# The second gate's column sums: from VectorE's multiply-adds to a ScalarE scale and a GpSimd add

## The chip, the core and the metric

The kernel runs on one core of a Trainium2 chip. The metric is the time of one execution on the device in microseconds (us), taken as the median of several runs. Five engines work side by side, each through its own queue of instructions in order: TensorE (PE: matmuls, with PEld for its weight loads), VectorE (DVE), ScalarE (ACT), GpSimd (POOL) and SyncE (SP, which here issues the loads). An instruction waits at the head of its queue until what it needs is there, and all behind it on that engine wait too.

## What is computed

One decoder block over 256 tokens of width 2048, all in float32. A conditioning vector c gives six vectors of 2048 numbers, and the last of them, the second gate g2, is what the change is about:

```python
mod = silu(c) @ w_ada + b_ada                      # (2048) @ (2048 x 12288)
sh1, sc1, g1, sh2, sc2, g2 = split(mod, 6)
h = rms_norm(x) * (1 + sc1) + sh1;  proj = h @ w_in
# ... attention on one half of the heads, a short gated convolution on the other
x = x + g1 * (mixed @ w_out)
h2 = rms_norm(x) * (1 + sc2) + sh2
u = causal_dwconv(h2 @ w_ffn_up);  u_gate, u_up = split(u, 2)
x = x + g2 * ((silu(u_gate) * u_up) @ w_ffn_down)
```

## The kernel before

**Slots.** The program is written as a row of slots. Each slot is one tile of weights (128 x 4 x 512 numbers, 1 MB) and the matmuls that use it. The slots are those of `w_in`, then `w_out`, then the feed-forward in four segments: of each segment the up projection (tiles named z) and then the down projection (tiles named m('D', segment, f)). A float32 weight tile is used as two halves: `split_hi` lets ScalarE write the upper half `hi` (L266), `split_lo` lets VectorE subtract it from the raw tile to get the lower half `lo` (L272). `hi` and `lo` have three buffers each. Slot i prepares the halves of slot i+2, so `lo` is made one to two slots ahead of the matmuls that read it.

**Loads.** Raw tiles (`raw`, six buffers) are loaded by SyncE in the order in which they will be used: when one has been used up, `load_next` issues the next load into the buffer that comes free.

**The six vectors (class Ada).** `w_ada` is loaded as raw tiles among the weights. A group of columns is summed up in one of two ways: on TensorE (L324), or as column sums on VectorE: for each of the 16 blocks of 128 rows, the tile times `csil` (one number per partition, silu(c)) is added to an accumulator of 128 partitions (L328, L330). Which slots take which tile is in a table (CFG['ada']). The second gate (part 5) is one group of 2048 columns: 16 tiles of 128 x 2048, each a raw tile of its own, spread over 21 slots from slot 103. Its accumulator takes one of the six raw buffers: `home` clears it on GpSimd and loads the bias into its row 0 (L308, L310). One multiply-add at L330 follows per tile.

**After the sums.** `halve` splits a quarter of the accumulator (512 columns) into halves, ScalarE (L347) and then VectorE (L348), and `spread` (L386, L387, L390) sums over the partitions with matmuls against ones. The first `halve` of the second gate stands in the slot after the last tile was added; the `spread`s come 21 slots later. Around it, in the up projection of the second segment, VectorE and ScalarE do the sums of a group (`up_sum`, L768, L771), its convolution (L734, L739) and its gating (L786, L790, L792, L793).

**The order inside slot i:** `split_hi` for slot i+2, the tasks of the slot, `split_lo` for slot i+2, the slot's matmuls, and then the Ada tiles of the slot (`consume`, L315). Some slots have `split_hi` after the tasks. No scheduler changes this: each engine runs its instructions as they are written.

Of the kernel before, what the change touches and what calls it, by code (L numbers as in the profile page):

```python
# [10 lines left out]
AF = mybir.ActivationFunctionType  # L11
ALU = mybir.AluOpType
# [15 lines left out]
SH1, SC1, G1, SH2, SC2, G2 = range(6)  # L28
# [106 lines left out]
def tile_block(  # L135
# [5 lines left out]
    nc = tc.nc  # L141
    mm = nc.tensor.matmul
    act = nc.scalar.activation
# [7 lines left out]
    def bank(name):  # L151
        return ps.tile([P, 512], F32, tag="b", bufs=8, name=name)
# [3 lines left out]
    def t2k(name, dt=F32):  # L156
        return sb.tile([P, 512], dt, tag="t2k", bufs=N_T2K, name=name)
# [7 lines left out]
    def t4k(name, dt=F32):  # L165
        return sb.tile([P, 1024], dt, tag="t4k", bufs=N_T4K, name=name)
# [61 lines left out]
    def load_next():  # L228
        if pending:
            if isinstance(pending[0], Ada):  # L230

                pending.pop(0).home()
                return
            t = sb.tile([P, 4, 512], F32, tag="raw", bufs=N_RAW, name="raw")
            pending.pop(0)(t)
            ready.append(t)

    def take():
        t = ready.pop(0)
        return t  # L240
# [36 lines left out]
    csil = const.tile([P, NK], F32, name="csil")  # L277
# [6 lines left out]
    class Ada:  # L284
# [30 lines left out]
        def consume(self, r):  # L315
            t = self.view(take())
            if r == 0 and self.acc is None:
                what = f"ada{self.part}_{self.c0}"
                self.acc = (bank(what) if self.pe else t4k(what) if self.n > 512 else t2k(what))[:, :self.n]
            for j in range(self.rows):  # L320
                i = self.rows * r + j
                if self.pe:
                    q = 32 * (j % 4)
                    mm(self.acc[q:q + 32, :], crep[:, i, :], t[:, j, :],  # L324
                       start=(r == 0 and j < 4), stop=(r == self.tiles - 1 and j >= self.rows - 4),
                       tile_position=(0, q))
                elif i == 0 and self.n <= 1024:
                    V.tensor_scalar(self.acc, t[:, j, :], csil[:, i:i + 1], None, op0=ALU.mult)  # L328
                else:
                    V.scalar_tensor_tensor(out=self.acc, in0=t[:, j, :], scalar=csil[:, i:i + 1],  # L330
                                           in1=self.acc, op0=ALU.mult, op1=ALU.add)
            load_next()
# [265 lines left out]
    for n, (f, part, k) in enumerate(seq):  # L598
# [6 lines left out]
        i = len(slots)  # L605
# [519 lines left out]
    for half in range(2):  # L1125
        for w in "qk":
            at(in_last[f"{w}{half}"], qk_stat, f"{w}{half}")
        i = max(in_last[f"{w}{half}"] for w in "qk")
# [274 lines left out]
```

## Time and profile before

| | |
|---|---|
| median of 3 runs | 1172.55 us (1172.13 to 1173.67) |
| span of the profiled execution | 1170.4 us |
| what the runs' median has beyond that span | 2.2 us |
| PE / PEld busy | 1151.1 / 973.6 us |
| DVE busy | 921.9 us |
| ACT busy | 626.3 us |
| POOL busy | 12.0 us |
| loads | 318 MB, mean 272 GB/s |

The page gives the span of one profiled execution, from its first instruction to its last; the runs' times lie 2.2 us above it. All comparisons of stretches below are in us from the start of that span. A row of a group reads: line, engine, operation, output<-inputs, shapes, count | busy us, mean ns of one | idle time of the engine just before them, and who ended it. A row of the timeline reads: start, duration, engine, line, operation; in brackets how long the engine was idle before it and what it waited for. Durations hold a small tail that overlaps with the next instruction of the same engine.

### The profile page before, as it was taken

The page shows a single profiled execution, that of the slowest core. Times are in us where ns is not written, and L with a number is a line of the kernel's source. Part 1 is how long each engine was busy: PE and PEld are TensorE (multiplying, and loading weights), DVE is VectorE, ACT ScalarE, POOL GpSimd, SP SyncE. Part 2 cuts the span into 40 slices and gives each one's busy share as a digit, 9 for nine tenths or more (in the row PEclk, how much of TensorE's full clock was granted, in tenths as well). Part 3 has the DMA queues.
Part 4 walks back from the last instruction along what each step waited for, and adds up shares of the span by engine and source line. Part 5 has one row for each costly group of instructions (what it writes and reads, how often), then busy time and mean ns, then how long its engine had stood idle before and what let it go on. Part 6 is the DMA issues. An engine that isn't in the chain of part 4 may idle for free.

```text
span 1170.4 us, 15668 instructions
## 1 busy us (share of the span) xinstructions
PE 1151.1 (98%) x6115; PEld 973.6 (83%) x6115; DVE 921.9 (79%) x1030; ACT 626.3 (54%) x906; POOL 12.0 (1%) x24
## 2 busy tenths in 40 slices
PE   5999999999999999999999999999999999999998
PEld 3777778888888889988888888888888888888886
DVE  3889989999999978899876767986556576478766
ACT  6645365567785564666664444555444554336441
POOL 1000000000000000000000000000000000000000
PEclk9999999999999999999999999999999999999999
DMA  9999989999899799975555898984664646675441
GB/s 364 406 415 411 409 321 372 378 349 347 287 332 350 251 326 331 359 253 178 186 194 168 305 337 301 310 279 154 208 222 159 201 162 216 222 252 168 150 162 73
DMA packets 189052, 318.00 MB, mean 272 GB/s; under 512 B 7073, under 2 KB 105845, under 8 KB 184625
## 3 DMA queue, kind: packets, MB, share of 16 engines
q1 hardware_dynamic: 187232, 314.60, 75.6%
q10 hardware_dynamic: 1296, 2.16, 0.5%
q8 instruction: 48, 0.79, 0.3%
q0 software_dynamic: 448, 0.24, 0.1%
q14 instruction: 28, 0.22, 0.1%
HBM read 312.77 MB, written 4.19 MB: 271 GB/s over the span
## 4 chain that ended last, share of the span: by engine, by line
PE 91%; DVE 3%; ACT 2%; DMA 2%; issue 1%; SPq 0%; DVEq 0%; ACTq 0%
PE z L875 24%; PE z L878 13%; PE z L861 4%; DVE lo L272 1%; PE ada L324 1%; PE mk L443 1%; PE mk L444 1%; PE mk L441 1%; PE mq L443 1%; PE mq L444 1%; PE mq L441 1%; PE mx L443 1%; PE mc L443 1%; PE mx L444 1%; PE mc L444 1%; PE mv L443 1%
## 5 line engine op out<-in xcount | busy, mean ns | idle before, releaser
L272 DVE TENSOR_TENSOR lo<-raw,hi 128x2048 fp32r<-128x2048 f32 (+2 forms) x201 | 445.9, 2224 | 140.4 <-ACT hi L266 135.5
L266 ACT ACTIVATE hi<-raw 128x2048 fp32r<-128x2048 f32 (+2 forms) x201 | 373.8, 1865 | 311.9 <-PE z L875 60.2
L875 PE MATMUL z<-h,hi 128*128 128x512 f32 x1280 | 299.0, 390 | 0.2 <-DVE h L696 0.2
L875 PEld LDWEIGHTS z<-h,hi 128*128 128x128 f32 x1280 | 237.6, 188 | 48.1 <-PE z L875 0.6
L330 DVE SCALAR_TENSOR_TENSOR ada<-raw,csil,ada 128x512 f32<-128x512 f32 (+3 forms) x167 | 195.4, 1175 | 5.6 <-DMA raw<-in_w_ada_dram 2.1
L878 PEld LDWEIGHTS z<-h,lo 128*128 128x128 f32 x1280 | 159.3, 192 | 3.4
L878 PE MATMUL z<-h,lo 128*128 128x256 f32 x1280 | 160.5, 283 | 0.0
L739 DVE SCALAR_TENSOR_TENSOR uy<-ub,fc,uy 128x254 f32<-128x254 f32 (+1 forms) x176 | 71.3, 476 | 0.2
L771 DVE TENSOR_TENSOR ub<-z,ub 128x256 f32<-128x256 f32 x96 | 33.9, 415 | 37.9 <-ACT ub L768 37.9
L792 ACT ACTIVATE gh<-uy 128x512 fp32r<-128x512 f32 x22 | 13.9, 632 | 62.9 <-DVE uy L790 62.9
L861 PE MATMUL z<-h,hi 128*128 128x256 f32 x256 | 46.6, 284 | 0.4 <-ACT h L693 0.2
L734 ACT ACTIVATE uy<-ub,fc,fc 128x256 f32<-128x256 f32 x88 | 45.6, 602 | 0.0
L768 ACT ACTIVATE ub<-z 128x256 f32<-128x256 f32 x96 | 28.8, 384 | 31.4 <-PE z L875 31.4
L861 PEld LDWEIGHTS z<-h,hi 128*128 128x128 f32 x256 | 40.0, 192 | 0.8 <-ACT h L693 0.5
L861 PE MATMUL z<-h,lo 128*128 128x256 f32 x128 | 36.2, 283 | 0.0
L324 PE MATMUL ada<-raw,crep 128*32 128x256 f32 (+1 forms) x192 | 20.3, 535 | 7.9 <-DMA raw<-in_w_ada_dram 7.9
L793 DVE TENSOR_TENSOR gl<-uy,gh 128x512 fp32r<-128x512 f32 x22 | 15.2, 692 | 15.4 <-ACT gh L792 15.4
L443 PE MATMUL mq<-hi,h 128*128 128x512 f32 x64 | 25.5, 398 | 0.4 <-DVE adaz L361 0.4
L443 PE MATMUL mx<-hi,h 128*128 128x512 f32 x64 | 25.7, 401 | 0.0
L443 PE MATMUL mc<-hi,h 128*128 128x512 f32 x64 | 25.6, 400 | 0.0
L443 PE MATMUL mk<-hi,h 128*128 128x512 f32 x64 | 25.1, 393 | 0.0
L443 PE MATMUL mv<-hi,h 128*128 128x512 f32 x64 | 25.1, 392 | 0.0
(612 smaller groups left out, 1885.4 us busy)
## 6 DMA issues: line engine op xcount, KB each, us to landing
raw<-in_w_ada_dram SPq DMA_DIRECT2D x96, 1024.0 KB, 6.8
raw<-in_w_ffn_up_dram SPq DMA_DIRECT2D x176, 512.0 KB, 4.5
raw<-in_w_in_dram SPq DMA_DIRECT2D x47, 1024.0 KB, 7.8
raw<-in_w_ffn_down_dram SPq DMA_DIRECT2D x28, 1024.0 KB, 5.0
raw<-in_w_out_dram SPq DMA_DIRECT2D x16, 1024.0 KB, 6.0
raw<-in_w_ffn_down_dram SPq DMA_DIRECT2D x20, 768.0 KB, 4.2
xr<-in_x_dram SPq DMA_DIRECT2D x2, 1024.0 KB, 6.4
x<-in_x_dram SPq DMA_DIRECT2D x8, 256.0 KB, 6.6
```

What stands on the lines that cost most here:

```text
L266: act(hi[:, :nk], t[:, :nk], AF.Copy)
L272: V.tensor_tensor(out=lo[:, :nk], in0=t[:, :nk], in1=hi[:, :nk].bitcast(F32), op=ALU.subtract)
L324: mm(self.acc[q:q + 32, :], crep[:, i, :], t[:, j, :], start=(r == 0 and j < 4), stop=(r == self.tiles - 1 and j >= self.rows - 4), tile_p ...
L330: V.scalar_tensor_tensor(out=self.acc, in0=t[:, j, :], scalar=csil[:, i:i + 1], in1=self.acc, op0=ALU.mult, op1=ALU.add)
L443: mm(o, a, hi[:, k, s], start=(first and k == 0), stop=False)
L444: mm(o, b, hi[:, k, s], start=False, stop=False)
L734: act(y[:, s], b[:, s], AF.Identity, bias=bias[:, i + j:i + j + 1], scale=w[2][:, i + j:i + j + 1])
L739: V.scalar_tensor_tensor(out=o[:, d:], in0=v[:, :256 - d], scalar=w[2 - d][:, i + j:i + j + 1], in1=o[:, d:], op0=ALU.mult, op1=ALU.add)
L771: V.tensor_tensor(out=d, in0=zp[grp][ft][:, :256], in1=d, op=ALU.add)
L861: mm(o, w[:, j, a], h2T[k + j][:, v * 256:v * 256 + 256], start=begins and j == 0 and w is hi and not v, stop=ends and j == 3 and w is lo)
L875: mm(zp[grp][ft], hi[:, j, ft * P:(ft + 1) * P], h2T[k + j], start=begins and j == 0, stop=ends and j == 3)
L878: mm(zp[grp][ft][:, :256], lo[:, j, ft * P:(ft + 1) * P], h2T[k + j][:, :256], start=False, stop=False)
```

## The change

For tiles of the second gate alone, `consume` issues two instructions in place of one: ScalarE multiplies the raw tile in place by silu(c), and GpSimd adds it to the accumulator. The accumulator, the loads, their order and everything after the sums stay as they are. Lines behind the change have numbers higher by 3 in the new kernel.

```diff
                 elif i == 0 and self.n <= 1024:
                     V.tensor_scalar(self.acc, t[:, j, :], csil[:, i:i + 1], None, op0=ALU.mult)
+                elif self.part == G2:
+                    act(t[:, j, :], t[:, j, :], AF.Copy, scale=csil[:, i:i + 1])
+                    nc.gpsimd.tensor_tensor(out=self.acc, in0=self.acc, in1=t[:, j, :], op=ALU.add)
                 else:
                     V.scalar_tensor_tensor(out=self.acc, in0=t[:, j, :], scalar=csil[:, i:i + 1],
                                            in1=self.acc, op0=ALU.mult, op1=ALU.add)
```

Two places show how the instructions move. The first is ScalarE's queue at the end of the sums, before the change; `adah` is the upper half that the first `halve` writes, `ada_0_5668` the accumulator, `ub` and `uy` are tiles of the up projection's sums and convolution, `gh` an upper half of the gated result:

```order
L266 ACTIVATE hi<-raw 128x2048
L734 ACTIVATE uy_6567<-ub_6506,fc_1676,fc_1672 128x256 x2
L734 ACTIVATE uy_6568<-ub_6507,fc_1676,fc_1672 128x256 x2
L266 ACTIVATE hi<-raw 128x2048 x2
L347 ACTIVATE adah<-ada_0_5668 128x512
L786 ACTIVATE uy_6567<-uy_6567 128x512
L792 ACTIVATE gh_6673<-uy_6567 128x512
L266 ACTIVATE hi<-raw 128x2048
```

The same stretch of ScalarE's queue after the change:

```order
L266 ACTIVATE hi<-raw 128x2048
L737 ACTIVATE uy_6581<-ub_6519,fc_1676,fc_1672 128x256 x2
L737 ACTIVATE uy_6582<-ub_6520,fc_1676,fc_1672 128x256 x2
L330 ACTIVATE raw<-raw,csil 128x2048
L266 ACTIVATE hi<-raw 128x2048
L330 ACTIVATE raw<-raw,csil 128x2048
L266 ACTIVATE hi<-raw 128x2048
L350 ACTIVATE adah<-ada_0_5668 128x512
L789 ACTIVATE uy_6581<-uy_6581 128x512
L795 ACTIVATE gh_6689<-uy_6581 128x512
L266 ACTIVATE hi<-raw 128x2048
```

The scales (now at L330) stand between the weight splits, each behind the `hi` of its own slot; the first `adah` is still behind all of them, and now it needs the last add of GpSimd. The second place is VectorE's queue at the same point, before:

```order
L330 SCALAR_TENSOR_TENSOR ada_0_5668<-raw,csil,ada_0_5668 128x2048
L272 TENSOR_TENSOR lo<-raw,hi 128x2048
L739 SCALAR_TENSOR_TENSOR uy_6567<-ub_6506,fc_1668,uy_6567 128x255 x2
L739 SCALAR_TENSOR_TENSOR uy_6567<-ub_6506,fc_1664,uy_6567 128x254 x2
L739 SCALAR_TENSOR_TENSOR uy_6568<-ub_6507,fc_1668,uy_6568 128x255 x2
L739 SCALAR_TENSOR_TENSOR uy_6568<-ub_6507,fc_1664,uy_6568 128x254 x2
L330 SCALAR_TENSOR_TENSOR ada_0_5668<-raw,csil,ada_0_5668 128x2048
L272 TENSOR_TENSOR lo<-raw,hi 128x2048
L330 SCALAR_TENSOR_TENSOR ada_0_5668<-raw,csil,ada_0_5668 128x2048
L348 TENSOR_TENSOR adal<-ada_0_5668,adah 128x512
L272 TENSOR_TENSOR lo<-raw,hi 128x2048
```

And VectorE's queue there after the change:

```order
L272 TENSOR_TENSOR lo<-raw,hi 128x2048 x2
L742 SCALAR_TENSOR_TENSOR uy_6581<-ub_6519,fc_1668,uy_6581 128x255 x2
L742 SCALAR_TENSOR_TENSOR uy_6581<-ub_6519,fc_1664,uy_6581 128x254 x2
L742 SCALAR_TENSOR_TENSOR uy_6582<-ub_6520,fc_1668,uy_6582 128x255 x2
L742 SCALAR_TENSOR_TENSOR uy_6582<-ub_6520,fc_1664,uy_6582 128x254 x2
L272 TENSOR_TENSOR lo<-raw,hi 128x2048
L351 TENSOR_TENSOR adal<-ada_0_5668,adah 128x512
L272 TENSOR_TENSOR lo<-raw,hi 128x2048
```

The multiply-adds are gone from VectorE and nothing else on it moved; `adal` still stands in front of a `lo`. GpSimd's queue had nothing behind the clearing and the bias load of this accumulator; now 16 adds of 128 x 2048 follow there, one behind the other.

## Prediction

> **What bounds the kernel now.** First the page, for the engines over the whole span:
>
> ```profile
> PE 1151.1 (98%) x6115; PEld 973.6 (83%) x6115; DVE 921.9 (79%) x1030; ACT 626.3 (54%) x906; POOL 12.0 (1%) x24
> ```
>
> TensorE is busy almost throughout. A share over the span says nothing of one stage, so the next view is the stretch in which the second gate is summed: from the first weight split beside the sums (650.77) to the matmuls that follow the last (769.98, explained below). The columns are us in the stretch, then PE, PEld, DVE, ACT and POOL busy, the clock, the DMA share and GB/s:
>
> ```profile
> 650.77:769.98 119.21, 119.21 (x625) 102.88 (x624) 95.86 (x66) 52.22 (x50) 0.00 (x0) 1.00 0.92 322
> ```
>
> TensorE never stops here (119.21 of 119.21 us, at the full granted clock). VectorE is busy 80% of it, ScalarE 44%, GpSimd not at all. So nothing that VectorE sheds can show in the time as long as TensorE has no wait: what counts is whether the change makes one. What TensorE needs from the others is the lower half `lo` of each weight tile, and VectorE's groups in this stretch show what shares its queue with `lo`:
>
> ```profile
> L272 DVE TENSOR_TENSOR lo<-raw,hi 128x2048 fp32r<-128x2048 f32 x21 | 48.0, 2287 | 17.9 <-ACT hi L266 17.9
> L330 DVE SCALAR_TENSOR_TENSOR ada<-raw,csil,ada 128x2048 f32<-128x2048 f32 x16 | 37.5, 2344 | 0.0
> L739 DVE SCALAR_TENSOR_TENSOR uy<-ub,fc,uy 128x255 f32<-128x255 f32 x8 | 3.5, 474 | 0.0
> L739 DVE SCALAR_TENSOR_TENSOR uy<-ub,fc,uy 128x254 f32<-128x254 f32 x8 | 3.5, 473 | 0.0
> L771 DVE TENSOR_TENSOR ub<-z,ub 128x256 f32<-128x256 f32 x8 | 2.8, 417 | 6.0 <-ACT ub L768 6.0
> L348 DVE TENSOR_TENSOR adal<-ada,adah 128x512 fp32r<-128x512 f32 x1 | 0.7, 693 | 0.7 <-ACT adah L347 0.7
> L793 DVE TENSOR_TENSOR gl<-uy,gh 128x512 fp32r<-128x512 f32 x1 | 0.7, 692 | 0.7 <-ACT gh L792 0.7
> L790 DVE TENSOR_TENSOR uy<-uy,uy 128x512 f32<-128x512 f32 x1 | 0.7, 679 | 0.0
> ```
>
> VectorE's timeline gives the rhythm at the start of the sums and at their end:
>
> ```profile
> 650.77 2.29 DVE L272 TENSOR_TENSOR lo<-raw,hi 128x2048 fp32r<-128x2048 f32 x1 [3.14 <-ACT hi L266]
> 652.99 2.35 DVE L330 SCALAR_TENSOR_TENSOR ada<-raw,csil,ada 128x2048 f32<-128x2048 f32 x1
> 656.22 2.29 DVE L272 TENSOR_TENSOR lo<-raw,hi 128x2048 fp32r<-128x2048 f32 x1 [0.89 <-ACT hi L266]
> ...
> 761.57 2.34 DVE L330 SCALAR_TENSOR_TENSOR ada<-raw,csil,ada 128x2048 f32<-128x2048 f32 x1
> 764.61 0.69 DVE L348 TENSOR_TENSOR adal<-ada,adah 128x512 fp32r<-128x512 f32 x1 [0.70 <-ACT adah L347]
> 765.22 2.29 DVE L272 TENSOR_TENSOR lo<-raw,hi 128x2048 fp32r<-128x2048 f32 x1
> ```
>
> A slot takes 5.45 us (650.77 to 656.22); a `lo` and a multiply-add fill 4.64 of it. The last `lo`, behind `adal`, ends at 767.51. TensorE's timeline says when it is due:
>
> ```profile
> 768.07 4.00 PE L878 MATMUL z<-h,lo 128*128 128x256 f32 x32
> 771.90 0.40 PE L875 MATMUL z<-h,hi 128*128 128x512 f32 x1
> ```
>
> These 32 matmuls read two lower halves, 16 each, and the second half of them begins in the middle, at (768.07 + 771.90) / 2 = 769.98. The `lo` that ends at 767.51 is the one for it, so VectorE is 2.5 us ahead of TensorE there. That is the tightest place in the stretch: the due time 769.98 is the end of the account below.
>
> **The change part by part.** *Removed:* 16 multiply-adds of 2.34 us, 37.5 us of VectorE. By itself worth nothing, as TensorE waits for nothing in this stretch.
>
> *Added on ScalarE:* 16 scales of 128 x 2048. The nearest row is its own weight split of that size, and the second row is the instruction that stands behind the sums:
>
> ```profile
> L266 ACT ACTIVATE hi<-raw 128x2048 fp32r<-128x2048 f32 x20 | 38.4, 1918 | 54.4 <-PE z L875 19.2 <-PE m('D', 0, 3)1_5903 L434 13.1 <-PE m('D', 0, 2)1_5868 L434 13.1
> L347 ACT ACTIVATE adah<-ada 128x512 fp32r<-128x512 f32 x1 | 0.6, 632 | 3.7 <-DVE ada L330 3.7
> ```
>
> And two rows of ScalarE's timeline, the eviction in front of the first scale and the `hi` of the tightest place:
>
> ```profile
> 651.12 0.59 ACT L810 ACTIVATE da<-m('D', 0, 0)1_5607 128x512 f32<-128x512 f32 x1
> ...
> 758.29 1.92 ACT L266 ACTIVATE hi<-raw 128x2048 fp32r<-128x2048 f32 x1 [2.79 <-DMA raw<-in_w_ffn_up_dram]
> ```
>
> 16 x 1.92 = 30.7 us, on an engine with 119.2 - 52.2 = 67 us free, 54.4 of them spent in front of `hi` waiting for TensorE to give a buffer back. The scale fits in that gap (`hi` 1.92 + scale 1.92 = 3.84 of 5.45 us a slot) and costs nothing; without the gap it would delay the next `hi`, behind which the ScalarE queue also holds the evictions of the up projection. Raw tiles are held longer: the first was free at 652.99 + 2.35 = 655.3, and now only when its add ends, about 3 us later; SyncE's queue is in order, so the weight load behind it is issued that much later. The `hi` of the tightest place waited 2.79 us for its load and began at 758.29; its `lo` may begin as late as 769.98 - 2.29 = 767.7, so this `hi` may begin 7 us later: such a load is covered.
>
> *Added on GpSimd:* 16 adds, two inputs of 128 x 2048 and one output. No row of before shows such an operation. What GpSimd did:
>
> ```profile
> 1.59 0.29 POOL L191 TENSOR_SCALAR_AFFINE_SELECT mask<-mask 128x128 f32<-128x128 f32 x1
> 174.38 1.82 POOL L308 MEMSET ada<- 128x2048 f32 x1 [79.16 <-DVE ada L330]
> 625.88 1.82 POOL L308 MEMSET ada<- 128x2048 f32 x1 [448.88 <-DVE lo L272]
> ```
>
> One pass of 128 x 2048, a write alone, takes 1.82 us. An add has three passes, two reads and a write. Lower bound: the reads follow each other and the write runs with them, 2 x 1.82 = 3.64 us. Upper bound: all three in turn, 5.46. The one row with an input (0.29 us for 128 columns) scaled by 16 gives 4.64, close to the middle; I take the middle, an estimate of 4.55 us. The Trainium skill (GPSIMD Engine Reference, Performance versus the Vector engine) gives 4497 ns for a GpSimd add of this size in float32; by that figure the sum below would be 0.8 us less.
>
> *Side by side, or in turns?* The adds are on an idle engine, and 16 x 4.55 = 73 us fit in 119. They cost nothing if GpSimd reads while VectorE reads. If the two must take turns whenever VectorE's instruction has two inputs in SBUF (as `lo`, L739, L790, L793 and L348 have), each add holds VectorE off like an instruction of its own, twice as long as the one removed. The trace of before cannot decide it, for GpSimd never reads beside VectorE there. It does show a GpSimd write beside such a VectorE instruction:
>
> ```profile
> 174.18 4.49 DVE L272 TENSOR_TENSOR lo<-raw,hi 128x2048 fp32r<-128x2048 f32 x2
> ```
>
> Two `lo` in 4.49 us, and the clearing at 174.38 took 1.82 us, as at 625.88: neither slowed the other, and this leaves the reads open. The Trainium skill (SBUF — State Buffer, Who interferes with whom) says that a VectorE instruction with two SBUF inputs contends with a GpSimd instruction that reads SBUF, not with one that only writes, and that the later one is held off whole; the clearing above agrees with the second half, no run here shows the first, and by it the sum would be the one for turns, without it zero. I forecast turns.
>
> *The sum, for turns.* What must pass one after the other from 650.77 until the last `lo` ends: 21 `lo` (48.0), the other VectorE work with two SBUF inputs (3.5 + 3.5 + 0.7 + 0.7 + 0.7 = 9.1), L771 (2.8; it reads PSUM, but stands in VectorE's queue), 16 adds (16 x 4.55 = 72.8), and `adah` between the last add and `adal` (0.6): 133.3 us. Two corrections: the first add can't start before the first scale has ended (651.12 + 0.59 + 1.92 = 653.6, where the first `lo` ends at 653.1: 0.6 us), and consecutive rows overlap by 2.29 - (652.99 - 650.77) = 0.07 us, 1.5 us for 21 `lo`. That leaves 132.4 us, for 119.2: the last `lo` is 13.2 us late, and TensorE with it. In rhythm: an add and a `lo` take 6.8 us where a slot has 5.45, so each slot with an add falls 1.4 us behind and uses up the lead of `lo`; the stalls come spread from the middle of the stretch on, the largest before the matmuls at 768. Behind them VectorE is free of sums and no lead is missing, but what TensorE lost is not won back, as it has no idle time to cut: 1172.55 + 13.2 = 1185.8 us. The profiled span, 1170.4, goes to 1183.6.
>
> With an add of 3.64 us the account closes at 132.4 - 14.6 = 117.8, under 119.2: no loss. With 5.46 it is 132.4 + 14.6 = 147.0: 27.8 us late, 1200.4 us.
>
> **The rivals.** *Side by side (no change):* GpSimd reads while VectorE reads. For it: the clearing beside `lo` cost nothing; against it: it read nothing. GpSimd then has one add per slot with time to spare, VectorE is emptier, TensorE is as full as before: 1172.6 us. It decides for "same" as long as the last add is done by 769.98 - 2.29 - 0.69 - 0.63 = 766.4; from the end of the first scale (653.6) that allows 112.8 / 16 = 7.05 us per add. Also in this result: turns with an add near the lower bound. *Adds over 7.05 us, side by side (slower):* then the first `halve` makes ScalarE wait for the last add, with the next `hi` behind it, and `adal` stops VectorE in front of the due `lo`. At 8 us an add this costs 16 x 0.95 = 15.2 us, 1187.8; a held raw tile would add to it. Against it: 5.46 is already three passes in turn. *Faster:* some wait of TensorE that VectorE's sums cause today would go. Against it: TensorE has none in the stretch, and after 769.98 the old VectorE was never behind. At the most it is a few tenths of a us. *The change does not do what it says:* the branch is reached for all 16 tiles, since the special case for i == 0 needs 1024 columns or fewer and this group has 2048; I give it nothing.
>
> **How the numbers follow.** A measurement of this kernel can tell some 0.2%, 2.3 us, from no change. Turns 0.66 (of it 0.04 so cheap that nothing shows), side by side 0.25, late adds 0.06, faster 0.03. So faster 0.03, same 0.29, slower 0.68. The predicted time is that of turns, 1185.8. The same result is too likely to be left out, so the range begins at 1172.0; it ends at 1196, an add of 5.2 us (16 x 0.65 = 10.4 more), which leaves out about 0.1 above and a few hundredths below. The range of turns by itself is 1172.6 to 1200.4.
>
> **What the profile of the changed kernel would show.** 16 adds on POOL (4.5 us each if I am right, with waits between); L272 in 650 to 785 with `lo` either longer than 2.29 us or kept idle with no `hi` to blame, starting as an add ends; adds and `lo` never overlapping in the timeline; waits of PE for `lo` of 13 us in all, the last in front of the first `halve`. I am wrong if `lo` keeps 2.29 us under a running add and PE shows no wait; then the time is 1172.6. If PE waits but `lo` and the adds do overlap, the cause is late adds or late loads.

## The result, and the profile after

The changed kernel takes 1185.44 us in the median (1184.49 to 1185.57, 4 runs) where the kernel before took 1172.40 in runs on the same chip: a ratio of 1.0108, 95% interval 1.0094 to 1.0122. It is 13.0 us slower; 1185.8 was forecast. The profiled span grew from 1170.4 to 1183.5 us.

The waits of TensorE in the stretch from 640 to 900 us of the changed kernel (who waited <- for whom: us in total, times, longest). Before there was no row here at all:

```profile
PE z L881 <- DVE lo L272: 8.5, 3, 4.6
```

TensorE's timeline of the same place. In brackets stands the idle time before a row; the 32 low matmuls took 4.00 us before:

```profile
738.49 7.44 PE L878 MATMUL z<-h,hi 128*128 128x512 f32 x32
748.80 5.59 PE L881 MATMUL z<-h,lo 128*128 128x256 f32 x32 [2.86 <-DVE lo L272]
754.22 7.44 PE L878 MATMUL z<-h,hi 128*128 128x512 f32 x32
761.50 2.07 PE L881 MATMUL z<-h,lo 128*128 128x256 f32 x16
764.63 2.18 PE L881 MATMUL z<-h,lo 128*128 128x256 f32 x16 [1.06 <-DVE lo L272]
766.65 7.44 PE L878 MATMUL z<-h,hi 128*128 128x512 f32 x32
778.71 6.47 PE L881 MATMUL z<-h,lo 128*128 128x256 f32 x32 [4.62 <-DVE lo L272]
```

The last block ends at 778.71 + 6.47 = 785.18, where it ended at 768.07 + 4.00 = 772.07 before: 13.1 us, the whole difference of the spans, within 40 us. Of it 2.86 + 1.06 + 4.62 = 8.5 us are waits for `lo`. Most of the rest is in the blocks themselves: 5.59 and 6.47 in place of 4.00, 4.1 us more. Windows of that place say why; the columns are as in the prediction, the share behind the engines is the granted clock of TensorE:

```profile
745.90:748.80 2.90, 0.04 (x1) 0.00 (x1) 2.90 (x4) 0.00 (x0) 0.00 (x0) 1.00 0.00 0
748.80:750.80 2.00, 2.00 (x14) 2.00 (x15) 2.00 (x1) 0.00 (x0) 0.00 (x0) 0.81 0.44 91
750.80:754.20 3.40, 3.40 (x20) 3.40 (x20) 1.44 (x3) 2.62 (x4) 0.00 (x0) 0.61 1.06 370
754.20:761.50 7.30, 7.30 (x34) 6.04 (x33) 6.28 (x6) 7.30 (x11) 4.37 (x1) 1.00 0.94 335
```

After the wait of 2.86 us the clock fell and came back. What was lost of it is 0.19 x 2.00 + 0.39 x 3.40 = 1.7 us, which at half clock (0.50 behind the last wait, a row further below) is some 3.4 us of reduced clock. So this wait of TensorE cost more than its own length.

Now the cause. VectorE's and GpSimd's groups after, in 650.77 to 785 and 640 to 790 us, to be set against the rows of before (`lo` 2287 ns, L739 474 ns):

```profile
L272 DVE TENSOR_TENSOR lo<-raw,hi 128x2048 fp32r<-128x2048 f32 x21 | 94.0, 4510 | 9.8 <-ACT hi L266 9.8
L742 DVE SCALAR_TENSOR_TENSOR uy<-ub,fc,uy 128x255 f32<-128x255 f32 x8 | 20.9, 2654 | 0.0
```

```profile
L331 POOL TENSOR_TENSOR ada<-ada,raw 128x2048 f32<-128x2048 f32 x16 | 96.0, 6003 | 49.4 <-ACT raw L330 48.7
```

Nothing in these instructions changed, yet `lo` takes twice as long. The time is a wait that the record counts as busy, and the ends show it. GpSimd's first adds and VectorE's `lo` beside them:

```profile
653.62 4.62 POOL L331 TENSOR_TENSOR ada<-ada,raw 128x2048 f32<-128x2048 f32 x1 [25.22 <-ACT raw L330]
664.95 6.55 POOL L331 TENSOR_TENSOR ada<-ada,raw 128x2048 f32<-128x2048 f32 x1
671.58 6.55 POOL L331 TENSOR_TENSOR ada<-ada,raw 128x2048 f32<-128x2048 f32 x1
```

```profile
650.71 2.29 DVE L272 TENSOR_TENSOR lo<-raw,hi 128x2048 fp32r<-128x2048 f32 x1 [3.14 <-ACT hi L266]
656.15 4.25 DVE L272 TENSOR_TENSOR lo<-raw,hi 128x2048 fp32r<-128x2048 f32 x1 [3.15 <-ACT hi L266]
666.98 13.29 DVE L272 TENSOR_TENSOR lo<-raw,hi 128x2048 fp32r<-128x2048 f32 x2
```

The first add had no competitor when it began: 4.62 us, until 658.24. The `lo` that was issued under it at 656.15 ended at 660.40, 2.16 us after the add's end: it did its whole work behind it. From then on both queues are full and the adds follow each other every 6.63 us (664.95, 671.58), one `lo` and one add, while two `lo` take 13.29 us. A slot has 5.45.

### The profile page after: what moved, and what is told of

It reads as the page before. It is cut to its first block, busy times and chain, and to the rows that moved or that the text cites. A ratio compares the mean times of both kernels' runs of the same rounds, so it can differ in the third digit from the quotient of the medians.

```text
span 1183.5 us, 15703 instructions
## 1 busy us (share of the span) xinstructions
PE 1155.6 (98%) x6115; PEld 977.4 (83%) x6115; DVE 949.5 (80%) x1014; ACT 657.0 (56%) x922; POOL 108.0 (9%) x40
## 3 DMA queue, kind: packets, MB, share of 16 engines
q10 hardware_dynamic: 1296, 2.16, 0.5%
## 4 chain that ended last, share of the span: by engine, by line
PE 85%; DVE 7%; DMA 4%; ACT 2%; issue 1%; SPq 0%; DVEq 0%; ACTq 0%
PE z L878 20%; PE z L881 11%; PE z L864 4%; DVE lo L272 4%; DMA raw<-in_w_ada_dram 2%; DVE uy L742 2%; PE mk L446 1%; PE mk L447 1%; PE mk L444 1%; PE ada L324 1%; PE mq L446 1%; PE mq L447 1%; PE mq L444 1%; ACT hi L266 1%; PE mc L446 1%; PE mx L446 1%
## 5 line engine op out<-in xcount | busy, mean ns | idle before, releaser
L272 DVE TENSOR_TENSOR lo<-raw,hi 128x2048 fp32r<-128x2048 f32 (+2 forms) x201 | 492.0, 2457 | 132.0 <-ACT hi L266 126.0
L881 PEld LDWEIGHTS z<-h,lo 128*128 128x128 f32 x1280 | 163.0, 196 | 12.8 <-DVE lo L272 9.6
L881 PE MATMUL z<-h,lo 128*128 128x256 f32 x1280 | 164.8, 287 | 8.5 <-DVE lo L272 8.5
L333 DVE SCALAR_TENSOR_TENSOR ada<-raw,csil,ada 128x512 f32<-128x512 f32 (+3 forms) x151 | 158.0, 1052 | 5.6 <-DMA raw<-in_w_ada_dram 2.1
L331 POOL TENSOR_TENSOR ada<-ada,raw 128x2048 f32<-128x2048 f32 x16 | 96.0, 6003 | 49.4 <-ACT raw L330 48.7
L742 DVE SCALAR_TENSOR_TENSOR uy<-ub,fc,uy 128x254 f32<-128x254 f32 (+1 forms) x176 | 88.8, 577 | 0.2
L774 DVE TENSOR_TENSOR ub<-z,ub 128x256 f32<-128x256 f32 x96 | 34.0, 416 | 32.9 <-ACT ub L771 32.9
L308 POOL MEMSET ada<- 128x2048 f32 x2 | 3.6, 1810 | 528.0 <-DVE lo L272 448.9
L864 PE MATMUL z<-h,lo 128*128 128x256 f32 x128 | 36.2, 283 | 0.0
L330 ACT ACTIVATE raw<-raw,csil 128x2048 f32<-128x2048 f32 x16 | 32.1, 2009 | 5.2 <-DMA raw<-in_w_ada_dram 4.9
L789 ACT ACTIVATE uy<-uy 128x512 f32<-128x512 f32 x22 | 13.8, 626 | 23.2 <-DVE uy L742 23.2
```

Source lines behind the costliest of these rows:

```text
L272: V.tensor_tensor(out=lo[:, :nk], in0=t[:, :nk], in1=hi[:, :nk].bitcast(F32), op=ALU.subtract)
L331: nc.gpsimd.tensor_tensor(out=self.acc, in0=self.acc, in1=t[:, j, :], op=ALU.add)
L742: V.scalar_tensor_tensor(out=o[:, d:], in0=v[:, :256 - d], scalar=w[2 - d][:, i + j:i + j + 1], in1=o[:, d:], op0=ALU.mult, op1=ALU.add)
L774: V.tensor_tensor(out=d, in0=zp[grp][ft][:, :256], in1=d, op=ALU.add)
L864: mm(o, w[:, j, a], h2T[k + j][:, v * 256:v * 256 + 256], start=begins and j == 0 and w is hi and not v, stop=ends and j == 3 and w is lo)
L881: mm(zp[grp][ft][:, :256], lo[:, j, ft * P:(ft + 1) * P], h2T[k + j][:, :256], start=False, stop=False)
```

## The experiments

Two theories were tried against each other. "Turns": a VectorE instruction with two inputs in SBUF and a GpSimd instruction that reads SBUF exclude each other, so the loss is a matter of rate and of the lead that `lo` has. "Longer path": what costs is the scale on ScalarE, the raw tiles held longer and the later last sum. "Before" in the ratios is the kernel before, run on the same chip. Source lines are those of each kernel.

**The adds on VectorE.** ScalarE's scales stay.

```diff
-                    nc.gpsimd.tensor_tensor(out=self.acc, in0=self.acc, in1=t[:, j, :], op=ALU.add)
+                    V.tensor_tensor(out=self.acc, in0=self.acc, in1=t[:, j, :], op=ALU.add)
```

> ScalarE's scales stay, and the 16 adds go to VectorE in place of GpSimd. Theory 'turns' (a VectorE instruction with two inputs in SBUF and a GpSimd instruction that reads SBUF exclude each other): without GpSimd nothing is excluded, VectorE has 16 adds of about 2.29 us where it had 16 multiply-adds of 2.34, so lo keeps 2.29 us, PE has no wait between 650 and 790, and the time is that of before, 1172.4 us within 1 us. Rival 'longer path' (the loss comes from the scale on ScalarE, from the raw tiles held longer and from the late last sum): the scale is still there, so at least a third of the 13 us stays, 1176 to 1185 us.

Measured 1173.01 us, ratio 0.9999 (0.9990 to 1.0009). The window 650 to 770 us of this kernel:

```profile
650.00:770.00 120.00, 120.00 (x625) 103.38 (x624) 95.11 (x66) 83.12 (x67) 0.00 (x0) 1.00 0.91 323
```

ScalarE is as busy as in the changed kernel (83.1 us here, 81.0 there in the same window), TensorE never stops. The scales cost nothing; the loss needs GpSimd.

**GpSimd writes and does not read.** The sums are left out.

```diff
-                    nc.gpsimd.tensor_tensor(out=self.acc, in0=self.acc, in1=t[:, j, :], op=ALU.add)
+                    for _ in range(3):
+                        nc.gpsimd.memset(t[:, j, :], 0.0)
+                    nc.gpsimd.memset(self.acc[:, :16], 0.0)
```

> In place of each add GpSimd clears the scaled raw tile three times (3 x 1.81 = 5.4 us, longer than the add's 4.5) and 16 columns of the accumulator: it writes SBUF and reads none. The sums are left out. Theory 'turns, by reading': lo keeps 2.29 us under a running clear, no wait of PE, 1172.4 us within 1 us. Rival 'longer path': GpSimd is busy for longer per tile than in the changed kernel and the tile comes free later, so the loss stays, 1180 to 1190 us. Rival 'any access to SBUF excludes': an account with 5.4 us per tile, 132.4 - 72.8 + 86.4 = 146 us in 119.2, 1195 us or more.

Measured 1172.78 us, ratio 1.0001 (0.9992 to 1.0010). The groups of GpSimd and of `lo` in 640 to 900 us:

```profile
L332 POOL MEMSET raw<- 128x2048 f32 x48 | 86.8, 1811 | 48.5 <-ACT raw L330 46.6
```

```profile
L272 DVE TENSOR_TENSOR lo<-raw,hi 128x2048 fp32r<-128x2048 f32 x41 | 93.7, 2290 | 69.4 <-ACT hi L266 69.4
```

GpSimd worked 86.8 us there, more than 16 adds alone would (16 x 4.62 = 74). It held each raw tile for 5.4 us, longer than an add alone would, though not quite as long as the adds with their waits (6.0). `lo` kept 2.29 us. So neither GpSimd's work as such nor tiles held that long cost the 13 us. Reading does.

**GpSimd reads one input.** The sums are left out; one run.

```diff
-                    nc.gpsimd.tensor_tensor(out=self.acc, in0=self.acc, in1=t[:, j, :], op=ALU.add)
+                    nc.gpsimd.tensor_copy(self.acc, t[:, j, :])
```

> In place of each add GpSimd copies the scaled tile over the accumulator: one input and one output. The sums are left out. Theory 'turns': one input in SBUF is enough to hold VectorE off, so lo that meets a running copy is recorded longer than 2.29 us and ends about 2.2 us after the copy's end; with a copy of 2 us the account is 132.4 - 72.8 + 32 = 91.6 us in 119.2, so PE does not wait and the time stays near 1172 us. If only two-input GpSimd instructions exclude, lo keeps 2.29 us.

Measured 1172.58 us. A copy takes 1.90 us alone, 2.24 in the mean, and `lo` and copies met only for short whiles. Where they did (a row of GpSimd, then one of VectorE):

```profile
725.62 2.58 POOL L331 COPY ada<-raw 128x2048 f32<-128x2048 f32 x1 [10.13 <-ACT raw L330]
```

```profile
727.33 3.01 DVE L272 TENSOR_TENSOR lo<-raw,hi 128x2048 fp32r<-128x2048 f32 x1 [0.90 <-ACT hi L266]
```

The copy ends at 728.20 and the `lo` at 730.34, 2.14 later. One input is enough to exclude; at this length there is room for both.

**Twelve of sixteen.** Every fourth tile stays with VectorE.

```diff
-                elif self.part == G2:
+                elif self.part == G2 and r % 4 != 3:
```

> Every fourth tile is summed by VectorE's multiply-add as before; 12 of 16 go by ScalarE and GpSimd. Theory 'turns': the account is 132.4 - 72.8 + 12 x 4.5 + 4 x 2.34 = 123.0 us in 119.2, so the last lo is about 4 us late instead of 13: 1174 to 1178 us. Rival 'longer path': the loss goes with the number of scaled tiles and with the last tile (which is now VectorE's): a quarter of it goes, 1180 to 1183 us.

Measured 1177.39 us, ratio 1.0034 (1.0021 to 1.0047): 4.3 us lost, a third of 13, where a quarter of the adds was taken back. One wait is left, and the 16 matmuls behind it took 3.68 us in place of 2.07:

```profile
PE z L881 <- DVE lo L272: 3.1, 1, 3.1
```

This fits the account for turns, in which a loss begins only where the sum of the turns exceeds the time: four adds given back as multiply-adds are worth 4 x (4.43 - 2.34) = 8.4 us by it (4.43 is an add as a turn, see below), and 13.0 - 4.3 = 8.7 were measured.

**Adds in four pieces.**

```diff
-                    nc.gpsimd.tensor_tensor(out=self.acc, in0=self.acc, in1=t[:, j, :], op=ALU.add)
+                    for h in range(0, 2048, 512):
+                        nc.gpsimd.tensor_tensor(out=self.acc[:, h:h + 512], in0=self.acc[:, h:h + 512],
+                                                in1=t[:, j, h:h + 512], op=ALU.add)
```

> Each add is cut into four of 512 columns. Theory 'turns': the turn is held for a piece of about 1.2 us instead of 4.5, so a lo is held off by 1.2 us at most and PE keeps its pace until the end of the sums; but the total that must pass in turns is no smaller (four fixed costs more per tile, 16 x 0.3 = 5 us), so GpSimd falls behind instead, and the first halve waits for its last add: the lost time moves to one long wait at the end of the sums, 1182 to 1195 us in all, with ScalarE waiting for POOL at L352 for over 10 us. If a short turn makes the exclusion cheap, 1173 to 1177 us.

Measured 1189.77 us, ratio 1.0141 (1.0126 to 1.0156). The time fell into the range, the way did not: ScalarE waited 0.3 us for the last add in front of the halves, not over 10, and TensorE waited 9.9 us for `lo`.

**Pieces, and the halves later.** The same, with the gate's halves and spreads six slots later.

```diff
-'ada': [... [5, 0, 2048, False, 103, 21], ...]
+'ada': [... [5, 0, 2048, False, 103, 21, 6], ...]
```

> The pieces, and the halves and spreads of this gate six slots (33 us) later. Theory 'turns': if what is late in the pieces alone is the last add in front of the first halve, this hides it, and the time comes near to that of before, 1172 to 1177 us; what is left is raw tiles that GpSimd holds while it is behind, and so late loads. If lo itself is still held off, it stays at 1180 us or more.

Measured 1185.42 us, ratio 1.0104 (1.0089 to 1.0119); TensorE waits 9.4 us for `lo`. The second branch of the expectation came: hiding the last add does not bring back the time, `lo` itself is held off. The 4.3 us gained on the pieces before are clock and not waits: the granted clock from 740 to 810 us is 0.95 here and 0.90 there.

Both kernels with pieces assumed that a short turn lets VectorE through. What this one shows instead (the piece in GpSimd's timeline, then a small instruction in VectorE's):

```profile
735.87 1.47 POOL L332 TENSOR_TENSOR ada<-ada,raw 128x512 f32<-128x512 f32 x1
```

```profile
736.12 1.51 DVE L744 SCALAR_TENSOR_TENSOR uy<-ub,fc,uy 128x255 f32<-128x255 f32 x1
```

With both queues full the turns go one for one, whatever an instruction's size: an instruction of 0.47 us waits for a piece and takes 1.5. The eight of them in front of a `lo` take 12 us in place of 3.2, as they did in the changed kernel, where two of the eight waited for a whole add each (the group of L742 above: 20.9 us for 8).

The turns are not all of it here. From 640 to 800 us of the first kernel with pieces VectorE also waited long for `hi`; it is 14.2 us in the changed kernel and 25.9 before:

```profile
DVE lo L272 <- ACT hi L266: 47.3, 16, 6.4
```

ScalarE in turn waited 22.3 us for loads in front of `hi`, against 2.8 before. GpSimd, recorded as busy for 118.0 us with the pieces (96.0 with whole adds), was behind and gave the raw tiles back late, so loads came late: the remainder that this expectation named. How the loss of the pieces divides between turns and late loads no run separates.

**Spread over 36 slots.**

```diff
-'ada': [... [5, 0, 2048, False, 103, 21], ...]
+'ada': [... [5, 0, 2048, False, 103, 36], ...]
```

> The changed kernel with the 16 tiles spread over 36 slots in place of 21. Theory 'turns': what counts is the rate. Two slots of 10.9 us take two lo and about one add, 2 x 2.2 + 4.5 = 8.9 us, so the lead of lo is never used up: no wait of PE, 1172.4 us within 1.5 us, though a lo that meets an add is still recorded as 4 to 6.7 us long. Rival 'longer path': each scaled tile costs what it cost, about 13 us stay, 1180 to 1186 us.

Measured 1179.75 us, ratio 1.0052 (1.0035 to 1.0068): half of the loss is gone, but the expectation, no wait at all, missed. One wait of TensorE is left in 640 to 900 us:

```profile
PE m('D', 1, 0)0_7098 L436 <- DVE gl L796: 4.7, 1, 4.7
```

No `lo` in the rest of the stretch made TensorE wait. But at 829 us the down projection, already under way, comes to the lower half of the last gated tile (`gl`), which has next to no lead: in the kernel before it ends at 829.10 and the matmul that reads it begins at 829.29. Here a `lo` in front of it was held off by an add.

**Tiles in earlier slots**, 11 of them in the down projection from slot 97 on.

```diff
+            if g.part == G2:
+                s = 97 + r * 4 // 3 if r < 11 else 113 + (r - 11) * 3
```

> The changed kernel with its 16 tiles in other slots: 11 of them from slot 97 on, three in four slots, where the down projection leaves VectorE the most room, the other five every third slot from 113 to 125; none near the end of the up projection at slot 132. Theory 'turns': in the down projection four slots of 21.8 us take four lo and three adds, 4 x 2.2 + 3 x 4.45 = 22.2, nearly even; in the up projection three slots of 16.7 us take 6.6 + 4.5 + about 4.5 of other work. The lead of lo is never used up: 1172.4 to 1175 us, PE waiting for 2 us at most in 600 to 850. If each scaled tile costs by itself, about 13 us stay: 1180 to 1186 us.

Measured 1179.99 us, ratio 1.0068 (1.0050 to 1.0086): missed. Three adds in successive slots were too many at once, and one held off the `lo` in front of another `gl`, 37 us into the down projection of the first segment:

```profile
PE m('D', 0, 2)0_5888 L438 <- DVE lo L272: 1.7, 2, 0.9
PE m('D', 0, 3)0_5920 L438 <- DVE lo L272: 1.2, 2, 0.9
PE m('D', 0, 0)0_5607 L436 <- DVE gl L796: 1.1, 1, 1.1
```

These are 4.0 us, where the median lost 7.8 and the profiled span 6.6 (1177.0 to 1170.4). The rows count too little. A wait is counted from the recorded end of the matmul before it, but matmuls that do not wait follow each other every 0.23 us, before that end. The place of the last row:

```profile
645.97 0.39 PE L438 MATMUL m('D', 0, 0)1_5608<-lo,gh 128*128 128x512 f32 x1
647.50 0.50 PE L436 MATMUL m('D', 0, 0)0_5607<-hi,gl 128*128 128x512 f32 x1 [1.14 <-DVE gl L796]
```

From start to start these are 1.53 us in place of 0.23, so 1.3 us were lost where the row says 1.1. Over the whole down projection, between a row of z that began 0.1 us later than before (607.18 and 607.07) and one that began 5.8 us later (703.54 and 697.76), TensorE lost 5.7 us, most of the 6.6.

**36 slots, the last four tiles behind the place at 829 us.**

```diff
+            if g.part == G2 and r >= 12:
+                s = 135 + r - 12
```

> The spread over 36 slots with one thing changed: the last four tiles, which stood around the end of the up projection (slots 130 to 136), are summed in slots 135 to 138, behind it. In the spread over 36 slots PE waited once, 4.7 us at 829 us, for the lower half of the last gated tile (gl), which was behind a lo that an add held off, and its clock was halved for 3.41 us after. Theory 'turns, and a place without lead': without an add there that wait and the slow clock go, 1172.4 to 1175 us. If the 7 us come from the number of scaled tiles, the held raw tiles or the late last sum, they stay: 1178 to 1182 us.

Measured 1182.53 us, ratio 1.0086 (1.0070 to 1.0102): missed, though the wait at 829 us is gone. Four adds stood in four successive slots of 4.1 us, too short for an add and a `lo`:

```profile
PE m('D', 1, 3)0_7333 L436 <- ACT hi L266: 2.6, 1, 2.6
PE m('D', 1, 3)0_7333 L438 <- DVE lo L272: 1.9, 2, 1.1
PE m('D', 1, 2)0_7291 L438 <- DVE lo L272: 1.2, 2, 0.9
```

The longest of them is the way of the rival "late adds": that `hi` stood in ScalarE's queue behind the first half, which waited 9.1 us for the last add.

**36 slots, only the two tiles next to that place moved.** The lag of the spreads is shortened so that they keep their place. The change of the spread to 36 slots, as above, is left out of this cut and of the one before.

```diff
- 'slag': [6, 21],
+ 'slag': [6, 16],
+            if g.part == G2 and r >= 14:
+                s = 139 + (r - 14) * 3
```

> The spread over 36 slots again, with only its last two tiles moved: from slots 134 and 136, on both sides of the one wait at 829 us, to slots 139 and 142, three slots apart in the down projection (the spreads of the gate keep their place, so their lag is 16 slots in place of 21). Four adds in four successive slots behind that place, tried before, did take the wait at 829 away but outran the short slots there (4.1 us each, an add and a lo being 6.2). Theory 'turns, by rate and by lead': two lone adds with 12 us between them fit, no wait of PE between 640 and 900 over 1 us, 1172.2 to 1174.5 us. If the 7 us of the spread kernel come from the number of scaled tiles or the held raw tiles, they stay: 1177 to 1181 us.

Measured 1173.81 us, ratio 1.0013 (1.0004 to 1.0023). The wait at 829 us is down to this:

```profile
PE m('D', 1, 0)0_7098 L436 <- DVE gl L796: 0.4, 1, 0.4
```

All 16 scales and all 16 adds are in this kernel, with `lo` still recorded at 2716 ns in the mean, and 13 us have become 1.4. The loss was never in the work, only in where it met VectorE. No version was faster than the kernel before, which had no wait here to give.

## Why the prediction was right, and where it was not

**The bound.** TensorE without a wait, so that 37.5 us less on VectorE bring nothing: right. With GpSimd only writing, VectorE was rid of the same 16 multiply-adds, and the time stayed at 1172.78 us.

**The scale.** 32.1 us for 16 (2.01 us each, 1.92 had been taken), hidden as forecast. Of the 54.4 us in front of `hi` that the prediction put down to TensorE, its row names TensorE for 45.4, and 2.8 were a load (the row of 758.29); the room was there all the same. Raw tiles did come later: scales and `hi` waited some 11 us for loads from 640 to 800 us, where it was 2.8 before. No wait of TensorE came from that: up to the ends of the two long waits VectorE was at work or held off without a pause, from 728.27 to 748.75 and from 758.84 to 778.66 us, and waited for no `hi`.

**Turns.** Shown three ways: the ends of `lo` 2.2 us behind the ends of adds, no effect of writes, an effect of a copy. The Trainium skill (SBUF — State Buffer, Who interferes with whom) states this rule, that two SBUF inputs on VectorE contend with a GpSimd instruction that reads and not with one that writes; the traces agree on both halves. The test that the prediction named for it, adds and `lo` that never overlap in the timeline, was put wrongly: the records do overlap, since the wait is counted as busy in both. By that sign the loss would have been put down to late adds or late loads. One has to look at the ends.

**The add.** 4.55 us estimated, 4.62 measured alone, and about 4.43 as a turn (6.63 between adds, less 2.20 for a `lo`). The Trainium skill's figure (GPSIMD Engine Reference, Performance versus the Vector engine), 4497 ns, agrees to 3%. That the middle of the two bounds came so near is luck: a copy, one read and one write, took 1.90 us, which by the count of passes speaks for the lower bound, 3.64.

**The sum.** 132.4 us of turns were forecast between the first `lo` and the end of the last; measured are 130.8 (650.71 to 781.46: the last two `lo` are the rows below).

```profile
776.38 2.28 DVE L272 TENSOR_TENSOR lo<-raw,hi 128x2048 fp32r<-128x2048 f32 x1
779.18 2.28 DVE L272 TENSOR_TENSOR lo<-raw,hi 128x2048 fp32r<-128x2048 f32 x1
```

So `lo` was 130.8 - 119.2 = 11.6 us late, 1.6 less than the 13.2 forecast; the size of the adds alone (4.43 as a turn for 4.55) makes 16 x 0.12 = 1.9 less. The 13.1 us of the spans need a term that the sum did not have: the slow clock behind the waits. TensorE did not even wait for that last `lo`. Its wait of 4.62 us ended with the `lo` before it (776.38 + 2.28 = 778.66), the block began 10.6 us later than before (778.71 and 768.07), and the slow clock made it 2.5 us longer. At that clock only 15 of its 32 matmuls had begun by 782.00 (the window of 778.70 further below), so it was still in the half that reads the earlier `lo` when the last one was done. The total was right partly by luck: less lateness than forecast and a cost of the clock that was not in the sum cancel. The forecast of "13 us of waits" failed in the same way: 8.5 are waits, 4.1 slow matmuls. The waits did come in the second half and the largest came last.

**Rivals.** Side by side is out, by the ends of `lo`. Late adds are out in the changed kernel: ScalarE did wait 4.1 us for the last add in front of the first half, but the `lo` after it had been held up before, and with the halves six slots later the pieces still lost 13 us. That the sum of turns over the stretch is the right account in the main is what the dose of twelve (3.8 us of lateness forecast by it, 4.3 measured, a part of them slow clock) and the last kernel show; what the sum leaves out, and the spread kernels taught, is that a place without lead must have no add near it at all.

**Left open.** How the loss of the kernels with pieces divides between turns and late loads; some 1 us of the kernel with the early tiles; and the last 1.4 us of the last one, of which 0.4 is a recorded wait.

## What to carry to other kernels

An idle GpSimd is no free second VectorE: each of its instructions that reads SBUF holds off VectorE's instructions with two SBUF inputs, here for 4.4 us per add where the multiply-add that it replaced took 2.3. If such work must go there, ask of the rate (turns per slot against the slot) and of the places without lead, not of the sum of busy times; cutting it into four pieces did not help (1189.77 us against 1185.44), as turns go one for one and the raw tiles were held longer. A moved instruction is worth nothing where TensorE has no wait, and waits that the move makes are paid with interest in clock, here those of 2.29 us and more.

## What the runs showed of the hardware that was not expected

**The clock falls after short waits.** A wait of 2.86 us brought about 3.4 us of reduced clock, as worked out above. Behind one of 4.62 the clock was 0.50 for 3.3 us, and the block of 32 low matmuls took 6.47 us in place of 4.00. The wait of 1.06 us did nothing (2.07 + 2.18 us for the two halves of the block). In the kernels with pieces one of 2.29 us was followed by a clock of 0.51 over 3.46 us, one of 2.13 us by 1.00.

```profile
778.70:782.00 3.30, 3.29 (x15) 3.29 (x16) 3.30 (x3) 0.00 (x0) 0.00 (x0) 0.50 0.66 187
```

The Trainium skill (TensorE: Matmul & The Clock Gate, What's actually happening) describes a gate that halves the clock after an idle window of about 3.4 us. The half clock and its length behind the first wait agree; the 2.86 and 2.29 us that sufficed here are shorter than such a window.

**An input in PSUM does not count.** The sums of the up projection (L774) have one input in PSUM and one in SBUF. In the kernel over 36 slots three of them ran under an add, GpSimd's row first:

```profile
813.37 4.62 POOL L331 TENSOR_TENSOR ada<-ada,raw 128x2048 f32<-128x2048 f32 x1 [0.65 <-ACT raw L330]
```

```profile
813.52 1.07 DVE L774 TENSOR_TENSOR ub<-z,ub 128x256 f32<-128x256 f32 x3
814.51 5.09 DVE L272 TENSOR_TENSOR lo<-raw,hi 128x1536 fp32r<-128x1536 f32 x1
```

Three took 1.07 us, their usual time, and the add its 4.62; the `lo` behind them, with two inputs in SBUF, waited until 817.99 and ended 1.6 us later.
